# Last group of W_down by eight plain products, and the first group's weight sums behind the norm

## The chip, the cores and the metric

The kernel runs on one core of a Trainium2 chip. The metric is device time in microseconds: the median of three executions. One further execution was recorded by the hardware profiler; all rows below come from that one.

## The reference, cut to what matters

Two decoder layers over 512 tokens of width 1024. Each layer mixes tokens (layer 0: differential and sparse attention, layer 1: forgetting attention), projects, adds and normalises, and then does the same with an MLP. What the change touches is the end of this:

```
x = layer_norm(ALPHA * x + mix, ...)                                   # first norm of a layer
x = layer_norm(ALPHA * x + square(relu(x @ w_up)) @ w_down, ...)       # second norm
```

`w_up` is 1024 x 4096 and `w_down` 4096 x 1024 per layer, all in float32. A float32 operand is used on TensorE as two parts, `hi` (rounded by ScalarE) and `lo` (the rest, a subtraction on VectorE or GpSimd), and a product is three matmuls: hi·hi, hi·lo, lo·hi.

## The kernel before, in words

Tokens lie in four tiles of 128; `xt_[t]` holds tile t of the residual stream with tokens on partitions, and `xTh`/`xTl` hold its transpose, split in two parts, which the projections read. The four engines have their own queues, worked off in order. The order inside each queue is not written by hand: a scheduler replays the program with a timing model of its own and queues, on each engine, what it finds ready, with the order of the source as the tie-break. A tile (a named buffer) that is asked for waits until one of its tag's buffers is free. All DMAs are issued from SyncE's queue (SP).

`out_proj` (L331) makes the first norm's input. Its second half (L355 to L363) goes token tile by token tile: for each t two PSUM banks (tag g, two buffers) of 24 matmuls of 256 columns, each drained by VectorE into `xt_[t]` (L361) with its statistics (L362), then `layer_norm`. Before that loop it already loads and splits the first half-chunk of W_up, `us0` (L346).

`layer_norm` (L207) aggregates the statistics on VectorE, takes the inverse root on GpSimd (L213), and normalises the two halves of the row: half 0 on VectorE (L223, L224), half 1 for tiles 0 to 2 on ScalarE and GpSimd (L219 to L221), for tile 3 on VectorE. Each half is then transposed on TensorE (L124) and split into `xTh`/`xTl` (L114 on ScalarE, L116 on VectorE), or, after the last norm, sent to the output.

`mlp` (L375) has four groups. In each, `up` makes two blocks of 512 hidden features (16 accumulations of 24 matmuls for the pair, in four half-chunks of weights; the first half-chunk of the first block reads tokens 0 to 383 and then 384 to 511), and `down` multiplies them with 1024 rows of W_down. `down` uses Winograd's form of Strassen's scheme: with H and W as 2 x 2 blocks, seven block products in place of eight, at the price of sums of blocks on VectorE: `left(r)` for H (L428 to L438), `right(r)` for W (L450 to L454, `wds` and `wdr` are the tiles). Every operand of a product is split in two (L407/L408 for W, L412/L413 for H). Products r = 3, 6, 7, 5, 1, 2, 4 run in that order, each for two row tiles tt; `evac` adds each to the rows of `xt_` it belongs to, or, for r = 3, to `E`, which goes into three of the four quarters at the very end (L495, last group alone). In the last group the products 2 and 4, which complete tiles 2 and 3, come last; the norms of tiles 0 and 1 are written ahead of them, those of 2 and 3 behind.

The W splits of W_up use tags `whi` and `wlo` (four buffers each) and the raw tag `wraw` (two buffers); W_down's raw blocks use `wdr` (eight buffers). After layer 0's second norm, layer 1 begins with a projection of 272 columns (`nat_chunk`, L181 to L183), 24 matmuls per token tile, whose weights come as three units through the same `wraw`, `whi` and `wlo`, the `lo` part on GpSimd (L146).

Of the kernel before, what the change touches and what calls it, by code (L numbers as in the profile page):

```python
# [15 lines left out]
P = 128  # L16
# [44 lines left out]
def tile_trunk(ctx: ExitStack, tc: tile.TileContext, x, xt_in, ln_gain, ln_bias, w_up, w_down, w_ie, w_oe, lam_p, subln,  # L61
# [46 lines left out]
    def new_xT():  # L108
        for k in range(2):
            xTh[k], xTl[k] = big(F32R), big(F32R)  # L110

    def split(src, hi, lo, scale=1.0):

        A.activation(hi, src, AF.Copy, scale=scale)  # L114
        if scale == 1.0:
            V.tensor_tensor(lo, src, hi.bitcast(F32), op=ALU.subtract)  # L116
        else:
            V.scalar_tensor_tensor(lo, src, scale, hi.bitcast(F32), op0=ALU.mult, op1=ALU.subtract)

    def transpose_x(t, half):  # L120
        b = bank("t")
        for k in range(4):
            c = (half * 4 + k) * P
            T.transpose(b[:, k * P:(k + 1) * P], xt_[t][:, c:c + P], ident)  # L124
        bv = b.rearrange("p (k c) -> p k c", k=4)
        split(bv, xTh[half][:, :, t * P:(t + 1) * P], xTl[half][:, :, t * P:(t + 1) * P])


    lo_engine, rope_engine = [V], [V]
# [77 lines left out]
    def layer_norm(pl, t, st, gb, bb, last=False, spill_to=None):  # L207
        y = xt_[t]
        mv = new(pl, "mv", [P, 2], bufs=2)
        V.bn_aggr(mv, st)  # L210
        ve = new(pl, "ve", [P, 2], bufs=2)
        V.tensor_scalar(ve[:, 0:1], mv[:, 1:2], EPS, None, op0=ALU.add)  # L212
        G.tensor_tensor(ve[:, 1:2], ve[:, 0:1], nhalf[:, 0:1], op=ALU.pow)  # L213
        if t < 3:
            V.tensor_scalar(ve[:, 0:1], mv[:, 0:1], ve[:, 1:2], -1.0, op0=ALU.mult, op1=ALU.mult)
        for hf in range(2):
            cs = slice(hf * 512, (hf + 1) * 512)
            if hf == 1 and t < 3:
                A.activation(y[:, cs], y[:, cs], AF.Identity, bias=ve[:, 0:1], scale=ve[:, 1:2])  # L219
                G.tensor_tensor(y[:, cs], y[:, cs], gb[:, cs], op=ALU.mult)  # L220
                G.tensor_tensor(y[:, cs], y[:, cs], bb[:, cs], op=ALU.add)  # L221
            else:
                V.scalar_tensor_tensor(y[:, cs], y[:, cs], mv[:, 0:1], gb[:, cs], op0=ALU.subtract, op1=ALU.mult)  # L223
                V.scalar_tensor_tensor(y[:, cs], y[:, cs], ve[:, 1:2], bb[:, cs], op0=ALU.mult, op1=ALU.add)  # L224
            if last:
                nc.sync.dma_start(out=out[t * P:(t + 1) * P, cs], in_=y[:, cs])
            else:
                transpose_x(t, hf)
                if spill_to is not None:
                    nc.sync.dma_start(out=spill_to[t * P:(t + 1) * P, cs], in_=y[:, cs])  # L230


    def stacks_q(ap, b, scale):
# [91 lines left out]
    def out_proj(pl, wo, mh, ml, kbs, ln, wu):  # L325

        for n in range(4):
            h, l = wo.take(256)
            for t0 in (0, 2):
                b = bank("g")  # L330
                bv = b.rearrange("p (b c) -> p b c", b=2)  # L331
                for tt in range(2):
                    ts_ = slice((t0 + tt) * P, (t0 + tt + 1) * P)
                    for k, kb in enumerate(kbs[:4]):
                        T.matmul(bv[:, tt], mh[kb][:, ts_], h[:, k], start=k == 0, stop=False)
                        T.matmul(bv[:, tt], mh[kb][:, ts_], l[:, k], start=False, stop=False)
                        T.matmul(bv[:, tt], ml[kb][:, ts_], h[:, k], start=False, stop=k == 3)
                for tt in range(2):
                    y = xt_[t0 + tt][:, n * 256:(n + 1) * 256]
                    V.scalar_tensor_tensor(y, y, ALPHA, bv[:, tt], op0=ALU.mult, op1=ALU.add)  # L340
        stats = [new(pl, f"st{t}", [P, 12]) for t in range(NT)]
        us = [wo.take(256) for _ in range(4)]
        us0 = wu.chunk(256, *[tuple(new(pl, tag, [P, 2, 2, 256], F32R, bufs=3).rearrange("p a b c -> p (a b c)")
                                    for tag in ("sh", "sl")) for _ in range(2)])
        new_xT()
        for t in range(NT):  # L346
            ts_ = slice(t * P, (t + 1) * P)
            for n in range(2):
# [12 lines left out]
                V.tensor_tensor(y, y, b, op=ALU.add)  # L361
                V.bn_stats(stats[t][:, n * 6:(n + 1) * 6], y)  # L362
            layer_norm(pl, t, stats[t].rearrange("p (a b) -> p a b", b=6), *ln)  # L363
        return us0

# [4 lines left out]

    def mlp(mp, wu, wd, us0, ln, last):  # L375
        stats = [new(mp, f"mst{t}", [P, 12]) for t in range(NT)]
        E = [new(mp, f"e{tt}", [P, 512]) for tt in range(2)]
        wdv = wd.flat.rearrange("(h c f p j e) -> h f p c j e", h=2, c=4, f=4, p=P, j=2)
# [1 line left out]
        def up(m):  # L380

            h = big()
            for j in range(2):
                us = us0 if m == 0 and j == 0 else wu.chunk(256, engs=(V, V))
# [30 lines left out]
        def down(g, hs, end):  # L415
# [64 lines left out]
            def evac(r, b, tt):  # L480
                y11, y12, y21, y22 = [Y(i, jd, tt) for i in range(2) for jd in range(2)]
                if r == 3:
                    if g == 0:
                        V.tensor_copy(E[tt], b)
                    else:
                        V.tensor_tensor(E[tt], E[tt], b, op=ALU.add)
                    return
                y = {6: y11, 7: y12, 5: y12, 1: y11, 2: y21, 4: y22}[r]
                op = ALU.subtract if r in (6, 7) else ALU.add
                if g == 0 and r in (6, 7, 2, 4):  # L490
                    V.scalar_tensor_tensor(y, y, ALPHA, b, op0=ALU.mult, op1=op)
                else:
                    V.tensor_tensor(y, y, b, op=op)
                if end and r in (5, 1, 4):
                    V.tensor_tensor(y, y, E[tt], op=ALU.add if r == 1 else ALU.subtract)  # L495

            def norm(t):
                for n in range(2):
                    V.bn_stats(stats[t][:, n * 6:(n + 1) * 6], xt_[t][:, n * 512:(n + 1) * 512])
# [3 lines left out]
            for r in (3, 6, 7, 5, 1) if end else (3, 6, 7, 5, 1, 2, 4):  # L503
                lf, us = left(r), right(r)
                for tt in range(2):
                    evac(r, product(r, lf, us, tt), tt)
            if end:
                if not last:
                    new_xT()
                rest = [(r, left(r), right(r)) for r in (2, 4)]  # L510
                for tt in range(2):
                    norm(tt)
                for tt in range(2):
                    for r, lf, us in rest:
                        evac(r, product(r, lf, us, tt), tt)
                    norm(2 + tt)

        for g in range(4):
            hs = [up(2 * g + m) for m in range(2)]
            down(g, hs, g == 3)  # L520


    def rope(ap, v, cos, sin, heads, bc):
# [473 lines left out]
    for layer in range(DEPTH):  # L997
        mh, ml, kbs, wo, src = (even_layer, odd_layer)[layer]()
        load_x(src)
        with ExitStack() as st:  # L1000
            mp = pool(f"mid{layer}", st)
            wu, wd = Weights(w_up[layer]), Weights(w_down[layer])
            ln = load_ln(mp, layer, 0)
            us0 = out_proj(mp, wo, mh, ml, kbs, ln, wu)
            ln = load_ln(mp, layer, 1)
            mlp(mp, wu, wd, us0, ln, layer == DEPTH - 1)


# [85 lines left out]
```

## Time and profile before

| | us |
|---|---|
| median of three executions | 1325.02 |
| lowest, highest | 1324.26, 1325.5 |
| the profiled execution | 1328.86 |
| its span, first to last instruction | 1326.7 |

Times in the rows are microseconds from the start of the span unless marked ns. PE is TensorE, DVE VectorE, ACT ScalarE, POOL GpSimd. "L12" is line 12 of the kernel before. A line of a timeline gives start, duration, engine, source line, operation, output <- input, count, and in brackets how long the engine had been idle and what released it. Matmuls are pipelined, so their durations overlap; the distance of their starts is what they cost.

### The profile page before, as it was taken

What the parts mean: (1) busy time and instruction counts of PE and PEld (TensorE: products, weight loads), DVE (VectorE), ACT (ScalarE), POOL (GpSimd) and SP (SyncE); (2) the same over time, 40 slices, a digit from 0 to 9 for tenths busy, and PEclk for the clock granted to TensorE, in tenths of its full rate; (3) what the DMA queues carried; (4) which work ended last, traced back from release to release, by engine and by line L of the source; (5) the groups of instructions that cost most, each with busy time, mean ns of one, the idle gap of its engine ahead of it and who ended that gap; (6) DMA issues with size and microseconds to landing.
All of it is one profiled execution on the core that took longest, in us unless ns stands there. A gap on an engine that the chain in (4) does not pass through costs nothing.

```text
span 1326.7 us, 18415 instructions
## 1 busy us (share of the span) xinstructions
PE 1245.3 (94%) x6998; PEld 1087.3 (82%) x6998; DVE 943.0 (71%) x1670; ACT 667.1 (50%) x1209; POOL 310.8 (23%) x321
## 2 busy tenths in 40 slices
PE   7999998999699999999978999999879999999994
PEld 7999896988688888888867789989868888888883
DVE  5467768786639578495796778878745947659488
ACT  5257767752245354454533576666325445354451
POOL 1135654454100000000054354556410000000003
PEclk9999998998799999999988999999979999999997
DMA  7321011225213405234022322232621431514201
GB/s 273 118 83 50 33 48 33 87 60 203 96 33 111 134 28 173 64 115 133 0 80 85 116 88 88 88 124 89 217 95 33 143 112 43 180 32 143 80 1 63
DMA packets 46760, 125.15 MB, mean 94 GB/s; under 512 B 4673, under 2 KB 5185, under 8 KB 46673
## 3 DMA queue, kind: packets, MB, share of 16 engines
q1 hardware_dynamic: 46672, 123.99, 28.4%
q8 instruction: 55, 0.90, 0.3%
q14 instruction: 33, 0.26, 0.1%
HBM read 119.75 MB, written 4.23 MB: 93 GB/s over the span
## 4 chain that ended last, share of the span: by engine, by line
PE 79%; DVE 7%; issue 5%; DMA 4%; POOL 3%; ACT 2%; SPq 0%; POOLq 0%; ACTq 0%; DVEq 0%
PE g L196 10%; PE g L194 10%; PE g L195 10%; PE g L181 4%; PE g L183 4%; PE g L182 4%; PE s L472 3%; PE s L473 3%; PE s L474 3%; PE t L288 3%; DMA wdr<-w_down 2%; PE o L473 2%; PE o L474 2%; PE t L472 2%; PE o L472 2%
## 5 line engine op out<-in xcount | busy, mean ns | idle before, releaser
L195 PE MATMUL g<-big,wlo 128*128 128x512 f32 x608 | 236.7, 391 | 0.0
L194 PE MATMUL g<-big,whi 128*128 128x512 f32 x608 | 236.6, 391 | 0.0
L196 PE MATMUL g<-big,whi 128*128 128x512 f32 x608 | 236.3, 390 | 0.0
L146 POOL TENSOR_TENSOR wlo<-wraw,whi 128x1024 fp32r<-128x1024 f32 (+2 forms) x51 | 126.3, 2481 | 428.8 <-ACT whi L145 416.4
L145 ACT ACTIVATE whi<-wraw 128x1024 fp32r<-128x1024 f32 (+3 forms) x120 | 125.1, 1045 | 130.5 <-DMA wraw<-w_up 45.6
L146 DVE TENSOR_TENSOR wlo<-wraw,whi 128x1024 fp32r<-128x1024 f32 (+2 forms) x69 | 84.5, 1227 | 138.8 <-ACT whi L145 138.8
L408 DVE TENSOR_TENSOR wlo<-wdr,whi 128x1024 fp32r<-128x1024 f32 x96 | 116.3, 1216 | 59.2 <-ACT whi L407 59.2
L407 ACT ACTIVATE whi<-wdr 128x1024 fp32r<-128x1024 f32 x96 | 101.3, 1055 | 64.3 <-PE t L474 37.6
L196 PEld LDWEIGHTS g<-big,whi 128*128 128x128 f32 x608 | 114.3, 188 | 23.6
L194 PEld LDWEIGHTS g<-big,whi 128*128 128x128 f32 x608 | 114.3, 188 | 23.5 <-issue 0.4
L195 PEld LDWEIGHTS g<-big,wlo 128*128 128x128 f32 x608 | 114.3, 188 | 23.1
L181 PE MATMUL g<-whi,big 128*128 128x256 f32 (+2 forms) x416 | 122.0, 293 | 1.4 <-ACT big L114 1.1
L183 PE MATMUL g<-whi,big 128*128 128x256 f32 (+2 forms) x416 | 121.8, 293 | 0.2 <-DVE ve L212 0.2
L182 PE MATMUL g<-wlo,big 128*128 128x256 f32 (+2 forms) x416 | 120.5, 290 | 0.0
L389 ACT ACTIVATE big<-g 128x512 f32<-128x512 f32 x64 | 38.3, 599 | 154.9 <-PE g L196 154.9
L275 ACT ACTIVATE p<-p,sm 128x128 f32<-128x128 f32 (+3 forms) x160 | 89.1, 558 | 46.0 <-DVE sm L274 45.0
L213 POOL TENSOR_TENSOR ve<-ve,nhalf 128x1 f32<-128x1 f32 x16 | 15.6, 974 | 362.2 <-DVE ve L212 362.2
L321 POOL TENSOR_TENSOR p<-p,rs 128x128 f32<-128x128 f32 (+2 forms) x108 | 71.4, 687 | 93.2 <-DVE rs L929 40.4
L181 PEld LDWEIGHTS g<-whi,big 128*128 128x128 f32 x416 | 80.6, 194 | 3.6 <-ACT big L114 1.9
L183 PEld LDWEIGHTS g<-whi,big 128*128 128x128 f32 x416 | 80.8, 194 | 1.2 <-DVE ve L212 0.5
L182 PEld LDWEIGHTS g<-wlo,big 128*128 128x128 f32 x416 | 80.7, 194 | 0.5
L116 DVE TENSOR_TENSOR ptl<-t,pth 128x384 fp32r<-128x384 f32 (+1 forms) x108 | 63.0, 595 | 21.9 <-ACT pth L114 21.3
(263 smaller groups left out, 3139.2 us busy)
## 6 DMA issues: line engine op xcount, KB each, us to landing
wraw<-w_up SPq DMA_DIRECT2D x64, 512.0 KB, 3.6
wdr<-w_down SPq DMA_DIRECT2D x64, 512.0 KB, 4.5
wraw<-w_io SPq DMA_DIRECT2D x22, 512.0 KB, 3.2
wraw<-w_ie SPq DMA_DIRECT2D x18, 512.0 KB, 3.5
v<-w SPq DMA_DIRECT2D x8, 512.0 KB, 5.8
wraw<-w_oe SPq DMA_DIRECT2D x8, 512.0 KB, 3.5
cb<-c_dram SPq DMA_DIRECT2D x16, 256.0 KB, 3.3
wraw<-w_oo SPq DMA_DIRECT2D x8, 512.0 KB, 3.2
```

Of the source, the lines that this page charges most:

```text
L145: A.activation(hi[:, c], raw[:, c], AF.Copy)
L146: (eng or lo_engine[0]).tensor_tensor(lo[:, c], raw[:, c], hi[:, c].bitcast(F32), op=ALU.subtract)
L181: T.matmul(bv[:, tt], xh, h, start=first, stop=False)
L182: T.matmul(bv[:, tt], xh, l, start=False, stop=False)
L183: T.matmul(bv[:, tt], xl, h, start=False, stop=last)
L194: T.matmul(b[:, a:e], h[:, cs], xh, start=k == 0, stop=False)
L195: T.matmul(b[:, a:e], l[:, cs], xh, start=False, stop=False)
L196: T.matmul(b[:, a:e], h[:, cs], xl, start=False, stop=k == 7)
L275: A.activation(pv, pv, AF.Exp, bias=sm[:, i:i + 1], scale=-1.0, accum_out=sm[:, 4 + i:5 + i])
L407: A.activation(hi, r, AF.Copy)
L408: V.tensor_tensor(lo, r, hi.bitcast(F32), op=ALU.subtract)
L472: T.matmul(bv, hh, us[m][0][:, k], start=first, stop=False, skip_group_check=True)
```

## The change

Two things change.

First, `transpose_x`, `layer_norm` and `out_proj` return the last VectorE instruction of the first norm, the subtraction L116 of tile 3's second half (`tail`). In the first block's second half-chunk of W_up, and in the first group's `right(r)`, every VectorE instruction gets an ordering edge behind `tail` (`tc.issue_after`). It is an edge in VectorE's queue alone: no semaphore is added, and the DMAs and the ScalarE casts of the same blocks are not held.

Second, groups 0 to 2 keep the seven products, and the last group becomes `down_last`: `E` goes into its three quarters first; the eight H parts and the eight W blocks are split without any sums; then, for each token tile t and each half jd of the output columns, 24 matmuls of 512 columns accumulate in one bank, VectorE adds the bank to `xt_[t]` and takes its statistics, and after both halves `layer_norm` of that tile follows. All split W blocks stay in their buffers until the last tile.

```
-            layer_norm(pl, t, stats[t].rearrange("p (a b) -> p a b", b=6), *ln)
-        return us0
+            tail = layer_norm(pl, t, stats[t].rearrange("p (a b) -> p a b", b=6), *ln)
+        return us0, tail
...
+                elif m == 0:
+                    with tc.issue_after(tail.ins):
+                        us = wu.chunk(256, engs=(V, V))
...
+            for r in (3, 6, 7, 5, 1, 2, 4):
+                lf = left(r)
+                if g == 0:
+                    with tc.issue_after(tail.ins):
+                        us = right(r)
...
+        def down_last(hs):
+            w = raws(3)
+            for tt in range(2):
+                for i, jd in ((0, 0), (0, 1), (1, 1)):
+                    y = xt_[2 * i + tt][:, jd * 512:(jd + 1) * 512]
+                    V.tensor_tensor(y, y, E[tt], op=ALU.add if jd == 0 else ALU.subtract)
+            H, U = {}, {}
+            for m in range(2):
+                for j in range(2):
+                    hi = new(mp, "sh" if m == 0 or j == 0 else "sl", [P, 2, SEQ], F32R, bufs=3)
+                    if m == 0:
+                        lo = new(mp, "sl", [P, 2, SEQ], F32R, bufs=3)
+                        lo = [lo[:, k] for k in range(2)]
+                    else:
+                        lo = [new(mp, f"t{2 + k}", [P, SEQ], F32R, bufs=2) for k in range(2)]
+                    for k in range(2):
+                        split(hs[m][:, 2 * j + k], hi[:, k], lo[k])
+                        H[m, j, k] = hi[:, k], lo[k]
+            for jd in range(2):
+                for m in range(2):
+                    for j in range(2):
+                        hi = new(wp, ("whi", "wlo")[j], [P, UW], F32R, bufs=4)
+                        lo = new(mp, "wdr" if U else "wds", [P, UW], F32R, bufs=8 if U else 2)
+                        split(w[f"{j + 1}{jd + 1}", m], hi, lo)
+                        U[jd, m, j] = [a.rearrange("p (c k e) -> p k c e", c=2, k=2) for a in (hi, lo)]
+            if not last:
+                new_xT()
+            for t in range(NT):
+                ts_ = slice(t * P, (t + 1) * P)
+                for jd in range(2):
+                    b = bank("os"[jd])
+                    bv = b.rearrange("p (c e) -> p c e", c=2)
+                    for m in range(2):
+                        for j in range(2):
+                            wh, wl = U[jd, m, j]
+                            for k in range(2):
+                                hh, hl = [a[:, ts_] for a in H[m, j, k]]
+                                T.matmul(bv, hh, wh[:, k], start=m + j + k == 0, stop=False)
+                                T.matmul(bv, hh, wl[:, k], start=False, stop=False)
+                                T.matmul(bv, hl, wh[:, k], start=False, stop=m + j + k == 3)
+                    y = xt_[t][:, jd * 512:(jd + 1) * 512]
+                    V.tensor_tensor(y, y, b, op=ALU.add)
+                    V.bn_stats(stats[t][:, jd * 6:(jd + 1) * 6], y)
+                layer_norm(mp, t, stats[t].rearrange("p (a b) -> p a b", b=6), *ln, last=last,
+                           spill_to=None if last else spill)
...
+        for g in range(3):
             hs = [up(2 * g + m) for m in range(2)]
-            down(g, hs, g == 3)
+            down(g, hs)
+        down_last([up(6 + m) for m in range(2)])
```

## Rows read from the trace of the kernel before

**Rows 1.** Parts 1 and 4 of the page: busy us and share; the chain.
```profile
span 1326.7 us, 18415 instructions
...
PE 1245.3 (94%) x6998; PEld 1087.3 (82%) x6998; DVE 943.0 (71%) x1670; ACT 667.1 (50%) x1209; POOL 310.8 (23%) x321
...
PE 79%; DVE 7%; issue 5%; DMA 4%; POOL 3%; ACT 2%; SPq 0%; POOLq 0%; ACTq 0%; DVEq 0%
```

**Rows 2.** Windows in the MLP: us; busy (xrecords) per engine; PEclk, DMA.
```profile
440.00:460.00 20.00, 20.00 (x90) 16.57 (x89) 4.91 (x4) 8.05 (x12) 0.00 (x0) 1.00 0.37 115
...
1280.00:1300.00 20.00, 19.85 (x88) 16.11 (x87) 20.00 (x29) 11.09 (x14) 0.00 (x0) 1.00 0.00 1
```

**Rows 3.** Timeline of PE, layer 0, into the MLP: start, us, instruction, [idle].
```profile
323.19 0.60 PE L124 MATMUL t<-ident,big 128*128 128x128 f32 x4
...
326.55 0.63 PE L124 MATMUL t<-ident,big 128*128 128x128 f32 x4 [1.69 <-issue]
...
343.95 1.09 PE L124 MATMUL t<-ident,big 128*128 128x128 f32 x4 [8.43 <-issue]
...
349.22 1.11 PE L124 MATMUL t<-ident,big 128*128 128x128 f32 x4 [1.85 <-POOL big L221]
```

**Rows 4.** DVE by line, layer 0, 320 to 350 us: busy, mean, idle.
```profile
L146 DVE TENSOR_TENSOR wlo<-wraw,whi 128x1024 fp32r<-128x1024 f32 x4 | 4.8, 1214 | 0.3 <-ACT whi L145 0.3
...
L450 DVE TENSOR_TENSOR wds<-wdr,wdr 128x1024 f32<-128x1024 f32 x2 | 3.5, 1761 | 1.9 <-DMA wdr<-w_down 1.9
...
L451 DVE TENSOR_TENSOR wdr<-wdr,wdr 128x1024 f32<-128x1024 f32 x2 | 3.3, 1665 | 0.0
```

**Rows 5.** The same of layer 1, 946 to 975 us.
```profile
L146 DVE TENSOR_TENSOR wlo<-wraw,whi 128x1024 fp32r<-128x1024 f32 x4 | 4.9, 1216 | 0.4 <-ACT whi L145 0.4
...
L450 DVE TENSOR_TENSOR wds<-wdr,wdr 128x1024 f32<-128x1024 f32 x2 | 3.6, 1836 | 0.6 <-DMA wdr<-w_down 0.6
...
L451 DVE TENSOR_TENSOR wdr<-wdr,wdr 128x1024 f32<-128x1024 f32 x2 | 2.3, 1207 | 0.0
```

**Rows 6.** Timeline of ACT: last evacuation of the first W_up half-chunk, both layers.
```profile
366.44 0.60 ACT L389 ACTIVATE big<-g 128x512 f32<-128x512 f32 x1 [2.94 <-PE g L196]
...
990.82 0.60 ACT L389 ACTIVATE big<-g 128x512 f32<-128x512 f32 x1 [3.35 <-PE g L196]
```

**Rows 7.** Windows at layer 0's MLP start: granted clock behind the busy times.
```profile
336.00:345.00 9.00, 1.05 (x4) 0.71 (x4) 8.73 (x17) 2.98 (x4) 1.99 (x3) 0.59 0.45 133
...
345.00:354.00 9.00, 6.42 (x22) 5.48 (x22) 6.70 (x7) 1.79 (x3) 4.09 (x2) 0.50 0.63 215
```

**Rows 8.** Part 5 of the page: the splits of W_down.
```profile
L408 DVE TENSOR_TENSOR wlo<-wdr,whi 128x1024 fp32r<-128x1024 f32 x96 | 116.3, 1216 | 59.2 <-ACT whi L407 59.2
...
L407 ACT ACTIVATE whi<-wdr 128x1024 fp32r<-128x1024 f32 x96 | 101.3, 1055 | 64.3 <-PE t L474 37.6
```

**Rows 9.** Timeline of PE, end of layer 0 and first projection of layer 1.
```profile
691.29 1.08 PE L124 MATMUL t<-ident,big 128*128 128x128 f32 x4 [7.58 <-DVE big L224]
...
718.58 0.39 PE L194 MATMUL g<-big,whi 128*128 128x512 f32 x1
```

**Rows 10.** Window inside that first projection at full clock.
```profile
714.50:718.50 4.00, 4.00 (x34) 4.00 (x33) 1.37 (x4) 2.46 (x4) 0.42 (x1) 1.00 0.00 0
```

**Rows 11.** Timeline of POOL at the end of layer 0.
```profile
684.51 1.83 POOL L146 TENSOR_TENSOR wlo<-wraw,whi 128x544 fp32r<-128x544 f32 x1 [1.65 <-ACT whi L145]
```

**Rows 12.** Timelines of DVE and POOL at the end of layer 1.
```profile
1304.64 2.46 DVE L499 BATCH_NORM_STATS2 mst<-big 128x6 f32<-128x512 f32 x4
...
1308.15 0.69 DVE L493 TENSOR_TENSOR big<-big,s 128x512 f32<-128x512 f32 x1 [0.27 <-PE s L474]
...
1308.82 0.74 DVE L223 SCALAR_TENSOR_TENSOR big<-big,mv,lng 128x512 f32<-128x512 f32 x1
...
1308.97 0.99 POOL L213 TENSOR_TENSOR ve<-ve,nhalf 128x1 f32<-128x1 f32 x1 [335.63 <-DVE ve L212]
...
1322.00 1.59 POOL L221 TENSOR_TENSOR big<-big,lnb 128x512 f32<-128x512 f32 x1
```

More of the change, by code (lines that the diff above doesn't have):

```diff
@@ L115, in split @@
         if scale == 1.0:
-            V.tensor_tensor(lo, src, hi.bitcast(F32), op=ALU.subtract)
-        else:
-            V.scalar_tensor_tensor(lo, src, scale, hi.bitcast(F32), op0=ALU.mult, op1=ALU.subtract)
+            return V.tensor_tensor(lo, src, hi.bitcast(F32), op=ALU.subtract)
+        return V.scalar_tensor_tensor(lo, src, scale, hi.bitcast(F32), op0=ALU.mult, op1=ALU.subtract)
     def transpose_x(t, half):
@@ L125, in transpose_x @@
         bv = b.rearrange("p (k c) -> p k c", k=4)
-        split(bv, xTh[half][:, :, t * P:(t + 1) * P], xTl[half][:, :, t * P:(t + 1) * P])
+        return split(bv, xTh[half][:, :, t * P:(t + 1) * P], xTl[half][:, :, t * P:(t + 1) * P])
     lo_engine, rope_engine = [V], [V]
@@ L227, in layer_norm @@
             else:
-                transpose_x(t, hf)
+                tail = transpose_x(t, hf)
                 if spill_to is not None:
                     nc.sync.dma_start(out=spill_to[t * P:(t + 1) * P, cs], in_=y[:, cs])
+        return None if last else tail
     def stacks_q(ap, b, scale):
@@ L362, in out_proj, with mlp @@
                 V.bn_stats(stats[t][:, n * 6:(n + 1) * 6], y)
-            layer_norm(pl, t, stats[t].rearrange("p (a b) -> p a b", b=6), *ln)
-        return us0
-    def mlp(mp, wu, wd, us0, ln, last):
+            tail = layer_norm(pl, t, stats[t].rearrange("p (a b) -> p a b", b=6), *ln)
+        return us0, tail
+    def mlp(mp, wu, wd, us0, tail, ln, last):
         stats = [new(mp, f"mst{t}", [P, 12]) for t in range(NT)]
@@ L383, in up @@
             for j in range(2):
-                us = us0 if m == 0 and j == 0 else wu.chunk(256, engs=(V, V))
+                if m == 0 and j == 0:
+                    us = us0
+                elif m == 0:
+                    with tc.issue_after(tail.ins):
+                        us = wu.chunk(256, engs=(V, V))
+                else:
+                    us = wu.chunk(256, engs=(V, V))
                 for nb in range(2):
@@ L413, in hsplit, with down @@
             V.tensor_tensor(lo, src, hi.bitcast(F32), op=ALU.subtract)
-        def down(g, hs, end):
+        def down(g, hs):
             H = [[[h[:, 2 * j:2 * j + 2, 256 * i:256 * i + 256] for j in range(2)] for i in range(2)] for h in hs]
@@ L493, in evac @@
                     V.tensor_tensor(y, y, b, op=op)
[L494 to L499, printed above, removed]
+            for r in (3, 6, 7, 5, 1, 2, 4):
[3 more added lines that the diff above has]
+                        us = right(r)
+                else:
+                    us = right(r)
+                for tt in range(2):
+                    evac(r, product(r, lf, us, tt), tt)
@@ new lines, in down_last @@
+        def down_last(hs):
+            w = raws(3)
+            for tt in range(2):
+                for i, jd in ((0, 0), (0, 1), (1, 1)):
[8 more added lines that the diff above has]
+                        lo = [lo[:, k] for k in range(2)]
+                    else:
+                        lo = [new(mp, f"t{2 + k}", [P, SEQ], F32R, bufs=2) for k in range(2)]
[27 more added lines that the diff above has]
+                    V.bn_stats(stats[t][:, jd * 6:(jd + 1) * 6], y)
@@ L500, in norm @@
                 layer_norm(mp, t, stats[t].rearrange("p (a b) -> p a b", b=6), *ln, last=last,
                            spill_to=None if last else spill)
[L503 to L516, printed above, removed]
@@ L518, in mlp @@
-        for g in range(4):
+        for g in range(3):
             hs = [up(2 * g + m) for m in range(2)]
-            down(g, hs, g == 3)
+            down(g, hs)
+        down_last([up(6 + m) for m in range(2)])
     def rope(ap, v, cos, sin, heads, bc):
@@ L1003, in tile_trunk @@
             ln = load_ln(mp, layer, 0)
-            us0 = out_proj(mp, wo, mh, ml, kbs, ln, wu)
+            us0, tail = out_proj(mp, wo, mh, ml, kbs, ln, wu)
             ln = load_ln(mp, layer, 1)
-            mlp(mp, wu, wd, us0, ln, layer == DEPTH - 1)
+            mlp(mp, wu, wd, us0, tail, ln, layer == DEPTH - 1)
 def _constants():
```

## The prediction, made blind

> **What bounds the kernel now.** I read the page first, then windows of 20 us over the whole span, then the timelines of the stretches in which TensorE has a gap. TensorE is busy for 1245.3 of the span's 1326.7 us, and the chain that ended last runs for 79% of the span through it [rows 1]. The reader is to see two kinds of stretch. Inside the MLP TensorE is full: 90 matmuls of 512 columns in 20.00 us, one per 0.222 us, and the same rate while VectorE too is busy all of the time [rows 2]. There, only the number of matmuls counts; a faster VectorE gives nothing. At four places TensorE stands still for a norm: at the start of each layer's MLP, at the end of layer 0, and at the end of the kernel. The change adds matmuls to the full stretch and touches all four gaps.
>
> **Added: matmuls of the last group.** Seven products of 2 x 12 matmuls are 168; four token tiles, two halves, 24 each are 192. 24 more at 0.222 to 0.227 us are 5.4 us per layer, 10.8 us in all, on the path in full.
>
> **Added and removed beside it, costed at nothing.** The last group's W splits fall from 14 blocks to 8: 8 x 1.06 us on ScalarE and 8 x 1.22 us on VectorE [rows 8], 8.4 and 9.7 us within the group's new 192 x 0.222 = 43 us; all block sums go. What hides them is `up`. The four blocks of the first output half take the weight buffers that the second block's first half-chunk gives back, half a block (48 matmuls, 10.9 us) before the products start, and need about 5 us of VectorE by then. The other four come free at the start of the products and are wanted 24 matmuls, 5.4 us, later, one per six matmuls (1.4 us). VectorE makes one in 1.2 us, so this just holds; if it doesn't, the price is a wait of 1 to 3 us per layer. I take 0.
>
> **Moved: the weight sums and subtractions at the start of the MLP.** In layer 0 VectorE ran four sums (3.5 + 3.3 us) and four subtractions of W_up (4.8 us) between the steps of the first norm, and stood 1.9 us waiting for W_down's transfer with the norm queued behind: 13.5 us, some 0.3 us less for the overlap of neighbours [rows 4]. In layer 1 it is 3.6 + 2.3 + 4.9 + 0.6 + 0.4 = 11.8 us [rows 5]. Four of these eight instructions per layer are subtractions, two of them of the next block; these aren't in the ordered blocks, but follow, as their raw data waits for one of two buffers that the first two give back. [...]
>
> With the moved work gone, what is late next is tile 2's second half. TensorE has its sums ready at 324.9 us (the 1.69 us of idle before 326.55 begin there [rows 3]). Sum, statistics and aggregate 1.7 us, inverse root 1.0 [rows 12], ScalarE's half row (taken like VectorE's, 0.74), GpSimd's two steps (1.6 each) [rows 12], transposes (0.60) [rows 3], split (0.60 like rows 6 and 0.69 like a sum [rows 12]), eight hand-overs of some 0.2: about 336 us. The first block then runs from 336 and not, after its false start, from the transposes at 349.22 [rows 3]. That would be 13 us or more, and a gap of some 4 us in place of 8.43 should leave less time at half clock. Against it stand the removed work as a cap on what VectorE's queue can give back (13.2 and 11.8 us) and a schedule that will not be ideal. I take 12 us for layer 0 and 11 us for layer 1. The bounds: 4 us each if another link (GpSimd's two steps, tile 3's own norm) holds TensorE nearly as long; 17 us each if the half clock goes with the gap. The marker is the last evacuation of the first half-chunk, at 366.44 and 990.82 us [rows 6].
>
> What waits for the moved work now: the second half-chunk's two subtractions (2.4 us behind the tail), wanted by TensorE only 96 matmuls after the block starts, some 12 us. SyncE's queue: W_up's next two raw blocks can be fetched only when these two have run, some 3 to 4 us later than now, and are wanted a whole block (22 us) later. The sums are for products 40 us away. All hidden; the price without that cover is what they cost now.
>
> **Moved: the norms at the end of layer 0.** Before, all four tiles complete in the last few microseconds of the products. TensorE's last product ends at 683.71 (691.29 less the 7.58 idle), and the next layer's first projection ends at 718.58 [rows 9]: 34.9 us, with 96 matmuls in it that take 4.00 / 34 = 0.12 us each at full clock [rows 10], some 12 us, and eight transposes. After, tiles 0 to 2 are normalised, transposed and split under the 10.9 us of the next tile's products. What is left behind the last matmul is tile 3: sum, statistics, aggregate 1.7 us, inverse root 1.0, four half-row steps of 0.74 [rows 12], transposes and split: 9 to 10 us, beside which the projection of tiles 0 to 2 (9 us) runs. Its weights: three units, of which GpSimd makes the short one in 1.83 us [rows 11], a long one by its size in 2.75. Now all three can be split only in the last 5.4 us, as the W blocks keep their buffers until tile 3; the third is ready some 4 to 5 us behind the last matmul. I put the end of the projection 16 us behind the last matmul: 34.9 - 16 = 18.9, less 5.4 added, a net gain of 13.5 us. Bounds 7 (GpSimd's splits hold tile 3's inverse root, half clock) and 15.
>
> **Moved: the norms at the end of the kernel.** The last sum starts at 1308.15, the last GpSimd step ends at 1323.59, and the span at 1326.7 [rows 12]: 15.4 us of four tiles' norms in a heap, 3.1 of transfer. After: sum and statistics 1.2 us, aggregate 0.3, inverse root 1.2 with a half-row step under it, two or three more at 0.7, some 4.3 us. 15.4 - 4.3 = 11.1, less 5.4, a net gain of 5.7. Bounds 3 and 7.
>
> **TensorE's queue in the last group.** Three tiles' transposes now stand between products of layer 0, and TensorE waits for them if they are placed too early. The same pattern is in `out_proj`, where it cost 1.69 us over the loop [rows 3]. I take 2 us. [...]
>
> **The sum.** -12 - 11 - 13.5 - 5.7 + 2 = -40.2 us, the 10.8 us of added matmuls included in the third and fourth terms. The profiled execution took 1328.86 us, 2.2 more than its span and 0.29% above the median of 1325.02. It would become 1288.7; against the median, 1325.02 - 40.2 = 1284.8 us.
>
> **Rivals.**
> *The starts give little.* VectorE's queue is cleared, but GpSimd's chain of tile 2 and tile 3's own norm end almost as late, and the clock is at half again. For it: the 1.85 us of idle before 349.22 ended at GpSimd's L221, not at VectorE [rows 3]. Against: that GpSimd step itself had waited for the VectorE steps ahead. With 4 us at each start: -8 - 13.5 - 5.7 + 2 = -25, 1300 us.
>
> [...]
>
> *The change doesn't do what it says.* If the edges only reorder what was late anyway, the starts give 0: -13.5 - 5.7 + 2 = -17, 1308 us. Against: all of the moved work was ahead of L116 in the queue, with no idle time but the transfer's [rows 4].
>
> **How the numbers follow.** My forecast has 0.66, the first rival 0.16, the third 0.07, the slower one 0.07; for a last group that loses just what the norms give, within 0.2% (2.65 us, what a measurement of this kernel can tell from no change), 0.04. Faster is 0.66 + 0.16 + 0.07 = 0.89. The forecast's own range comes from the bounds: at best -17 - 17 - 15 - 7 = -56, at worst -4 - 4 - 7 - 3 + 6 = -12; as they won't meet at one end, I take 1270 to 1304, which holds the first rival's time as well and leaves out the third and the slower one.
>
> **What would show it.** The evacuations of rows 6 some 11 to 12 us earlier against the start of their `out_proj`; no L450 or L451 on VectorE before the last L116; 192 matmuls in the last group at 0.222 us with no gap above 2 us; at most 17 us from the last product of layer 0 to the end of the first projection; about 8 us from the last matmul to the end of the span. I would be wrong if TensorE's gap at the start of the MLP stays above 6 us, or if gaps open between the token tiles.

## The result and the profile after

The changed kernel takes **1273.05 us** (median of 4 runs, 1272.16 to 1273.65) against 1325.26 (1324.26 to 1326.95) for the kernel before in the same session: ratio 0.9604, 95% interval 0.9588 to 0.9621. That is 52.2 us faster; 40.2 were forecast. A second set of runs gave 1275.20 us, ratio 0.9620 (0.9603 to 0.9636). Two slow executions are left out of what follows: 1373.98 us of `sums_only`, and 4320.5 us of the kernel before in the same session.

Parts 1 and 4 of the page after, against [rows 1]: TensorE is busy for 7.8 us less, although it runs 48 more matmuls, so part of its busy time before was slow time (mean granted clock over the span 0.964 before, 0.994 after). VectorE loses 65 us.
```profile
span 1271.5 us, 18398 instructions
...
PE 1237.5 (97%) x7046; PEld 1079.2 (85%) x7046; DVE 878.2 (69%) x1602; ACT 647.3 (51%) x1185; POOL 301.2 (24%) x321
...
PE 86%; DVE 6%; DMA 3%; ACT 2%; issue 1%; POOL 1%; SPq 0%; DVEq 0%; ACTq 0%; POOLq 0%
...
L414 DVE TENSOR_TENSOR wlo<-wdr,whi 128x1024 fp32r<-128x1024 f32 x72 | 87.4, 1218 | 44.4 <-ACT whi L413 44.4
...
L413 ACT ACTIVATE whi<-wdr 128x1024 fp32r<-128x1024 f32 x72 | 75.9, 1055 | 48.2 <-PE t L480 29.6
```
The last two lines answer to [rows 8]: 12 splits per layer fewer, and two more per layer from `wds`, which [rows 8] and these lines leave out. The last group's eight now run through `split` (L116), so eight stand for 14.

**The start of layer 0's MLP.** TensorE's timeline, against [rows 3]: the 8.43 us gap is gone. TensorE stands for 1.00 us, runs four matmuls of `up`, transposes tile 2's second half at 330.61, and then has matmuls without a break.
```profile
328.10 0.60 PE L123 MATMUL t<-ident,big 128*128 128x128 f32 x4
329.70 0.44 PE L193 MATMUL g<-big,sh 128*128 128x384 f32 x1 [1.00 <-ACT big L114]
...
330.61 0.66 PE L123 MATMUL t<-ident,big 128*128 128x128 f32 x4
...
337.18 1.03 PE L123 MATMUL t<-ident,big 128*128 128x128 f32 x8
```
VectorE's timeline, against [rows 4]: the sums (L456, L457) and the subtractions (L145) now stand behind the norm's last step, L116 at 338.45.
```profile
338.45 1.29 DVE L116 TENSOR_TENSOR big<-t,big 128x512 fp32r<-128x512 f32 x2 [4.50 <-ACT big L114]
339.65 2.35 DVE L145 TENSOR_TENSOR wlo<-wraw,whi 128x1024 fp32r<-128x1024 f32 x2
341.92 2.35 DVE L456 TENSOR_TENSOR wds<-wdr,wdr 128x1024 f32<-128x1024 f32 x2
344.19 2.35 DVE L457 TENSOR_TENSOR wdr<-wdr,wdr 128x1024 f32<-128x1024 f32 x2
```
Windows of the same place, against [rows 7] (the granted clock is the third number from the end): 1.00 where 0.59 and 0.50 stood.
```profile
336.00:345.00 9.00, 9.00 (x74) 8.97 (x73) 6.55 (x7) 2.15 (x4) 0.00 (x0) 1.00 0.42 124
345.00:354.00 9.00, 9.00 (x41) 7.45 (x41) 3.81 (x4) 4.93 (x8) 0.00 (x0) 1.00 0.44 142
```
ScalarE's evacuations, against [rows 6], are 20 us (layer 0) and 49 us (layer 1) earlier on the clock of the span; counted from token tile 1 of their `out_proj`'s second half it is 17.2 and 15.8 us, for the forecast's 11 to 12.
```profile
346.02 0.58 ACT L395 ACTIVATE big<-g 128x512 f32<-128x512 f32 x1
...
941.53 0.58 ACT L395 ACTIVATE big<-g 128x512 f32<-128x512 f32 x1
```

**The last group and the ends.** TensorE's timeline in layer 0: tile 0's transposes at 643.76 stand among the products of the next tile, with no idle time; behind the last product (670.46) it stands twice for 0.4 us, and the next layer's first projection ends at 685.13, 14.7 us behind, against 34.9 [rows 9].
```profile
643.76 0.60 PE L123 MATMUL t<-ident,big 128*128 128x128 f32 x4
...
677.34 1.29 PE L123 MATMUL t<-ident,big 128*128 128x128 f32 x8 [0.39 <-DVE big L223]
679.03 0.36 PE L180 MATMUL g<-whi,big 128*128 128x272 f32 x1 [0.41 <-DVE fz L946]
...
685.13 0.40 PE L193 MATMUL g<-big,whi 128*128 128x512 f32 x1
```
VectorE at the end of the kernel, against [rows 12]: one tile's norm, 4.6 us, where four stood.
```profile
1263.71 0.69 DVE L553 TENSOR_TENSOR big<-big,s 128x512 f32<-128x512 f32 x1 [4.13 <-PE s L551]
...
1266.87 1.41 DVE L223 SCALAR_TENSOR_TENSOR big<-big,ve,lnb 128x512 f32<-128x512 f32 x2
```

**Where the 55.2 us between the two spans lie,** by markers on TensorE and ScalarE: 3.2 ahead of token tile 1 in the second half of layer 0's `out_proj` (its 49th matmul), a stretch which the change doesn't touch (the profile before had more half clock there, see the last section); **18.1** from there to the third evacuation of `up` (layer 0's start); 12.1 from there to the end of layer 1's first projection (20.2 less behind the last product, 8.1 more in the products); 0.0 in layer 1's attention; **16.8** at layer 1's start; 4.9 to the end (10.8 less behind the last product, 5.9 more ahead of it). Without the untouched stretch it is 52.0, which is what the runs show.

### The profile page after: what moved, and what is told of

Its sections match the earlier page's. It is cut to its first block, busy times and chain, and to the rows that moved or that the text cites. A ratio compares the mean times of both kernels' runs of the same rounds, so it can differ in the third digit from the quotient of the medians.

```text
span 1271.5 us, 18398 instructions
## 1 busy us (share of the span) xinstructions
PE 1237.5 (97%) x7046; PEld 1079.2 (85%) x7046; DVE 878.2 (69%) x1602; ACT 647.3 (51%) x1185; POOL 301.2 (24%) x321
## 4 chain that ended last, share of the span: by engine, by line
PE 86%; DVE 6%; DMA 3%; ACT 2%; issue 1%; POOL 1%; SPq 0%; DVEq 0%; ACTq 0%; POOLq 0%
PE g L193 11%; PE g L194 11%; PE g L195 11%; PE g L180 4%; PE g L181 4%; PE g L182 4%; PE s L478 3%; PE t L288 3%; PE s L479 3%; PE s L480 2%; DMA wraw<-w_up 2%; PE s L270 2%; PE o L480 2%; PE t L478 2%; PE o L478 2%; PE o L479 2%
## 5 line engine op out<-in xcount | busy, mean ns | idle before, releaser
L145 DVE TENSOR_TENSOR wlo<-wraw,whi 128x1024 fp32r<-128x1024 f32 (+2 forms) x69 | 84.3, 1228 | 96.5 <-ACT whi L144 96.4
L145 POOL TENSOR_TENSOR wlo<-wraw,whi 128x1024 fp32r<-128x1024 f32 (+2 forms) x51 | 123.4, 2425 | 94.6 <-ACT whi L144 82.3
L180 PE MATMUL g<-whi,big 128*128 128x256 f32 (+2 forms) x416 | 120.3, 289 | 0.6 <-DVE fz L946 0.4
L182 PE MATMUL g<-whi,big 128*128 128x256 f32 (+2 forms) x416 | 119.6, 287 | 0.0
L414 DVE TENSOR_TENSOR wlo<-wdr,whi 128x1024 fp32r<-128x1024 f32 x72 | 87.4, 1218 | 44.4 <-ACT whi L413 44.4
L413 ACT ACTIVATE whi<-wdr 128x1024 fp32r<-128x1024 f32 x72 | 75.9, 1055 | 48.2 <-PE t L480 29.6
L180 PEld LDWEIGHTS g<-whi,big 128*128 128x128 f32 x416 | 79.1, 190 | 2.2 <-ACT fv L114 0.6
L182 PEld LDWEIGHTS g<-whi,big 128*128 128x128 f32 x416 | 79.1, 190 | 0.7 <-issue 0.4
L116 DVE TENSOR_TENSOR ptl<-t,pth 128x384 fp32r<-128x384 f32 (+1 forms) x108 | 63.1, 595 | 21.1 <-ACT pth L114 20.4
```

What stands on the lines that cost most here:

```text
L145: (eng or lo_engine[0]).tensor_tensor(lo[:, c], raw[:, c], hi[:, c].bitcast(F32), op=ALU.subtract)
L180: T.matmul(bv[:, tt], xh, h, start=first, stop=False)
L182: T.matmul(bv[:, tt], xl, h, start=False, stop=last)
L413: A.activation(hi, r, AF.Copy)
L414: V.tensor_tensor(lo, r, hi.bitcast(F32), op=ALU.subtract)
```

## The experiments

### Each half of the change alone

`order_only` keeps the last group of before and adds the two waits; `last_only` is the changed kernel without them:
```diff
 # order_only (both layers): seven products in the last group, but
+    with tc.issue_after(tail.ins): us = wu.chunk(256, engs=(V, V))   # m == 0, j == 1
+    with tc.issue_after(tail.ins): us = right(r)                     # g == 0
 # last_only: down_last as in the change, but
-    with tc.issue_after(tail.ins): ...
```


> Only the ordering edges of the change: the next half-chunk's subtractions and the first group's sums of W_down behind the preceding norm, in both layers; the last group stays seven products as before. Theory: the edges alone made the two starts shorter, by 18.1 us in layer 0 and 16.8 us in layer 1 of the two profiles, so about 1325 - 35 = 1290 us, and TensorE's clock stays at 1.00 behind out_proj. Rival: the starts gain only the 23 us of the forecast (1302 us), and the other 12 us of the result belong to the new last group (its buffers, and transfers that start earlier). The point between them is 1296 us.

Measured 1289.89 us, ratio 0.9732 (0.9718 to 0.9745): 35.2 us from the waits alone. In its profile the two starts are 41.2 and 41.9 us long (59.7 and 58.4 before, see the table below), so they account for all of it.

> Only the new last group: eight plain products, token tile by token tile, with the norms between them; no ordering edges, so both starts of the MLP stay as before. Theory: the end of layer 0 gives 12.2 us net and the end of the kernel 4.9 us net, 17 us, so about 1308 us, and with the edges' 35 us it adds up to the whole change's 52 us. Rival: the two parts help each other (the edges give buffers and transfers an earlier start), then this alone gives less than 12 us and the sum of both parts stays below 47 us.

Measured 1310.74 us, ratio 0.9890 (0.9877 to 0.9904): 14.3 us, a little under the 17. The product of the two ratios is 0.9625; the whole change had 0.9604 and 0.9620. The halves add up, and neither needs the other.

### Each wait alone

```diff
 # chunk_only: only the subtractions of W_up wait     # sums_only: only the sums of W_down wait
-    with tc.issue_after(tail.ins): us = right(r)      -    with tc.issue_after(tail.ins): us = wu.chunk(...)
```


> The changed kernel with one of its two ordering edges: the next half-chunk's subtractions of W_up wait for the preceding norm, the first group's sums of W_down don't. The two edges together gave 35.2 us. Theory: both kinds of moved work stood in VectorE's queue between the norm's steps, so each gives back in proportion to its time there: subtractions 4.8 of 13.2 us in layer 0 and about as much in layer 1, so this edge alone gives 35.2 x 0.38 = 13 us and leaves the kernel some 22 us above the changed one, at about 1295 us. Rival: the gap closes only when the last late step goes, so that one edge alone gives little (under 6 us: above 1302 us) and the two together more than their parts.

> The changed kernel with the other edge alone: the sums of W_down for the first group wait for the norm, the subtractions of W_up don't. Theory: in proportion to VectorE's time (8.4 of 13.2 us, the wait for the transfer included) it gives 35.2 x 0.62 = 22 us and leaves the kernel some 13 us above the changed one, at about 1286 us. Rival: the sums are nearly all of it (over 30 us, below 1278 us), because only they wait for a transfer with the norm behind them.

Measured 1301.11 us (0.9823; 0.9809 to 0.9837) and 1280.58 us (0.9670; 0.9651 to 0.9689). Against `last_only`, which has neither, that is 9.6 and 30.2 us; shares by VectorE's time would have been 13 and 22. Both kernels also lose 3.2 us in layer 1's attention, which they don't touch (222.6 and 222.5 us for 219.4; see `less24`), so the starts alone are to be compared: by the table below they are 11.3 us shorter in `chunk_only` than in `last_only`, 31.2 in `sums_only`, and 35.2 with both waits. The sums' wait by itself gives nine tenths, as its rival said, and the two parts alone add up to more than both give together. That the transfer is the reason, as that rival has it, is not shown. TensorE's timeline of `chunk_only` still has a long gap, its window the half clock:
```profile
337.04 1.09 PE L123 MATMUL t<-ident,big 128*128 128x128 f32 x4 [5.07 <-issue]
```
```profile
336.00:345.00 9.00, 6.52 (x24) 5.24 (x25) 7.59 (x10) 2.61 (x4) 4.00 (x4) 0.54 0.32 118
```
The same in `sums_only`: gaps of 0.69 and 1.02 us, and the full clock.
```profile
330.28 0.44 PE L195 MATMUL g<-big,sh 128*128 128x384 f32 x1 [1.02 <-DVE big L116]
```
```profile
336.00:345.00 9.00, 8.69 (x69) 8.28 (x68) 6.58 (x8) 2.01 (x4) 0.00 (x0) 1.00 0.46 160
```

### The gap filled, the wait left

```diff
 # warm: the kernel before, in out_proj behind the last product
+                with tc.issue_after(mm.ins):
+                    for _ in range(36):
+                        T.matmul(b, mh[kbs[0]][:, 0:P], mh[kbs[0]], start=True, stop=True)
```


> The kernel before, with 36 extra matmuls of 512 columns per layer into a bank that nobody reads, right behind out_proj's last product: 36 x 0.22 = 8 us of TensorE work in the place where TensorE stood idle for 8.43 us. VectorE's queue stays as it was, and so does the time at which the first block's inputs are ready. [...] Rival: the start is bounded by VectorE's queue throughout, and a faster clock there gives only another wait: 0 to -2 us, or slower by what the extra matmuls hold up.

Measured 1322.74 us, ratio 0.9982 (0.9974 to 0.9991): 2.4 us faster by the ratio, near the rival's end; the author's estimate for a clock that stays at 1.00 was 10 us. TensorE works through the former gap, and the window that had 0.50 has 0.81:
```profile
334.47 7.31 PE L367 MATMUL s<-big 128*128 128x512 f32 x31
...
345.66 0.44 PE L196 MATMUL g<-big,sh 128*128 128x384 f32 x1 [1.79 <-DVE big L116]
```
```profile
345.00:354.00 9.00, 8.34 (x42) 8.01 (x43) 3.80 (x7) 1.69 (x3) 1.13 (x1) 0.81 0.42 150
```
In the profile the two starts are 3.1 and 1.8 us shorter, 5 in all, and everything from there on is as before; why the timed runs show only half of it stays open (the execution behind the profile before took 1328.86 us, 3.8 more than the median). So extra work can buy back part of the clock, but the waiting itself has to go.

### The first block made to wait for tile 2's second half

The forecast had the first block start only when this half is there, at 336 us. In the changed kernel it starts earlier, on the first halves. Here the same matmuls run in the other order:
```diff
 # second_first, tr_block, first half-chunk only
-            for k in range(8):
+            for k in (4, 5, 6, 7, 0, 1, 2, 3):
```


> The changed kernel with one thing altered in each layer: the first block of the MLP (token tiles 0 to 2 in one piece, tile 3 in another, two output blocks) takes the second half of the model's columns before the first, with the same matmuls. So TensorE can't start it before tile 2's second half is there, which is what the forecast had assumed. [...] If the second half is there as early as the first, nothing is lost: 1273 us, and the forecast's 336 us was itself wrong.

Measured 1279.94 us, ratio 0.9662 (0.9644 to 0.9680), 4.7 us above the changed kernel beside it. The author's estimates of the loss were 7 us without a half clock behind the wait and 12 us with one; there is none, and each start carries only 1.7 us. The profile has another 3.1 us in layer 1's attention, where the scheduler placed other instructions. TensorE's timeline: three waits of 2.26 us together, and the clock stays at 1.00.
```profile
332.04 0.66 PE L123 MATMUL t<-ident,big 128*128 128x128 f32 x4 [1.15 <-POOL big L220]
333.38 0.44 PE L193 MATMUL g<-big,sh 128*128 128x384 f32 x1 [0.69 <-ACT big L114]
...
334.77 0.45 PE L195 MATMUL g<-big,sh 128*128 128x384 f32 x1 [0.42 <-DVE big L116]
```
Counted from token tile 1 of `out_proj`'s second half, 334.77 here is 335.8 in the profile before: the forecast's 336. The time of that half was right, and the early start on first halves is worth 1.7 us.

**A sum that holds in all of these.** From token tile 1 of `out_proj`'s second half to the third evacuation of `up` (whose pair of blocks has 8 accumulations of 24 matmuls, not the 16 of the description of the kernel): idle is the stretch less TensorE's busy time; clock is the sum over slices of 1 us of busy time x (1 - granted clock); the rest is work at full clock (of `warm` less its 36 x 0.222 = 8.0 us). In layer 0 it runs from 312.23 to 371.95 before, and from 309.00 to 350.65 after:
```profile
312.23 0.39 PE L357 MATMUL g<-whi,big 128*128 128x256 f32 x1 [0.31 <-DVE big L361]
...
371.95 0.60 ACT L389 ACTIVATE big<-g 128x512 f32<-128x512 f32 x1 [4.26 <-PE g L196]
```
```profile
309.00 0.39 PE L357 MATMUL g<-whi,big 128*128 128x256 f32 x1 [0.30 <-DVE big L361]
...
350.65 0.60 ACT L395 ACTIVATE big<-g 128x512 f32<-128x512 f32 x1 [2.58 <-PE g L195]
```
All stretches, in us:

| kernel | layer 0: length = idle + clock + rest | layer 1 |
|---|---|---|
| before | 59.7 = 12.9 + 5.7 + 41.1 | 58.4 = 13.2 + 4.3 + 40.9 |
| last_only | 59.7 = 12.9 + 5.7 + 41.1 | 58.8 = 13.4 + 4.6 + 40.9 |
| warm, less 8.0 | 48.6 = 5.2 + 1.7 + 41.7 | 48.5 = 5.6 + 1.5 + 41.4 |
| chunk_only | 54.0 = 9.7 + 2.9 + 41.4 | 53.2 = 8.7 + 3.5 + 40.9 |
| sums_only | 43.3 = 2.0 + 0.0 + 41.3 | 44.0 = 2.4 + 0.0 + 41.6 |
| second_first | 43.2 = 2.3 + 0.0 + 41.0 | 43.5 = 2.5 + 0.0 + 41.0 |
| after | 41.7 = 1.0 + 0.0 + 40.7 | 41.6 = 1.1 + 0.0 + 40.5 |

The rest stays between 40.5 and 41.7, so idle and clock carry the differences.

### The last group: overlap, matmuls, order

```diff
 # norms_late: the changed kernel, down_last
-                layer_norm(mp, t, ...)                    # behind each tile
+            with tc.issue_after(end.ins):                 # the last tile's bn_stats
+                for t in range(NT): layer_norm(mp, t, ...)
```


> The changed kernel, but the norms of all four token tiles of the last group wait until the last tile's statistics are there; the products, splits and sums stay as they are. Theory: what the last group gives at its ends is that three norms lie under the next tile's products. Without that, layer 0 pays again the 34.9 - 14.7 = 20 us less 2.6 us of transposes that leave the products' stretch, and the kernel's end 18.6 - 7.8 = 11 us: +28 us, about 1301 us. Rival: the gain comes from VectorE and ScalarE, which have 14 blocks to split before and 8 now and no block sums, and are free when the last product ends; then late norms cost half or less, +14 us, 1287 us. The point between them is 1294 us.

Measured 1299.89 us, ratio 0.9809 (0.9796 to 0.9823): 26.8 us lost, some 3 of them in layer 1's attention (222.5 us for 219.4): nearer the theory's 28 than the rival's 14. TensorE waits for the heap of norms again:
```profile
673.84 1.12 PE L123 MATMUL t<-ident,big 128*128 128x128 f32 x4 [5.40 <-DVE big L223]
...
678.63 0.59 PE L182 MATMUL g<-whi,big 128*128 128x272 f32 x1 [2.17 <-DVE big L116]
```
From the last product to the end of the first projection it is 29.2 us (14.7 in the changed kernel, 34.9 before), behind the kernel's last product 18.5 (7.8, and 18.6 before). VectorE has eight blocks to split and no sums here too. So the overlap makes 14.5 of the 20.2 us at layer 0's end and nearly all of the 10.8 at the kernel's. The other 5.7 us at layer 0's end are there without it; what gives them is not shown.

```diff
 # pool_lo: order_only, last group
-            V.tensor_tensor(lo, r, hi.bitcast(F32), op=ALU.subtract)
+            (G if end and m else V).tensor_tensor(lo, r, hi.bitcast(F32), op=ALU.subtract)
```


> The kernel before with the two ordering edges, the last group still seven products with its norms in two pairs, but the low parts of half of the last group's split weight blocks made on GpSimd in place of VectorE. This measures the rival for the ends: that VectorE's relief in the last group, not the tile by tile order, made its gain. Rival: with about 8 us of VectorE's subtractions gone from the last group, the kernel gains at least half of the 17 us that separate the edges alone (1290 us) from the changed kernel, that is below 1282 us. Theory: VectorE is not what the ends wait for until the last sums are there; no gain, 1288 to 1292 us, or slower where GpSimd is late with a block.

Measured 1293.87 us, ratio 0.9770 (0.9753 to 0.9786): 4.0 us slower than the waits alone. It is no test of the rival, as VectorE got no relief. In layer 0's last group 7 of 14 subtractions went to GpSimd, where they take 18.2 us; but VectorE's other steps grew beside them, and over the products it was busy for 37.73 of 38.64 us in `order_only` and 43.58 of 44.91 here (the third busy time of the windows). `order_only`:
```profile
624.05:662.69 38.64, 38.48 (x169) 31.27 (x167) 37.73 (x53) 20.34 (x27) 6.11 (x2) 1.00 0.03 8
L419 DVE TENSOR_TENSOR sl<-t,sh 128x512 fp32r<-128x512 f32 x6 | 4.0, 687 | 0.0
```
`pool_lo`:
```profile
624.66:669.57 44.91, 40.48 (x171) 32.63 (x170) 43.58 (x52) 21.33 (x28) 20.97 (x10) 0.96 0.02 7
L419 DVE TENSOR_TENSOR sl<-t,sh 128x512 fp32r<-128x512 f32 x6 | 9.5, 1593 | 0.1
```
The products now stand for blocks. In layer 0 that makes them 6 us longer, which the stretch behind the last product gets back (27.5 us for 34.0); in layer 1 it makes them 4 us longer, and nothing comes back:
```profile
643.44 0.47 PE L478 MATMUL s<-whi,sh 128*128 128x512 f32 x1 [2.30 <-ACT sh L418]
...
661.94 0.50 PE L479 MATMUL s<-wlo,sh 128*128 128x512 f32 x1 [2.12 <-DVE wlo L414]
```

```diff
 # less24: the changed kernel, down_last; tiles 0 to 2 without hl x wh of the first block
+    if m or t == 3:
         T.matmul(bv, hl, wh[:, k], start=False, stop=m + j + k == 3)
```


> The changed kernel without the low-part products of the first 1024-row block of the last group for token tiles 0 to 2 (8 matmuls in each of the tiles, 24 per layer, 48 in all; the output lacks these small terms). All else stays. Theory: TensorE is full in the last group, so each matmul there is on the path: 48 x 0.224 = 10.8 us less, 1262 us. Rival: the tile by tile order leaves slack behind splits or norms that hides some of them; then less than 6 us are saved, above 1267 us.

Measured 1264.82 us, ratio 0.9541 (0.9528 to 0.9554): 8.2 us saved, between the two. The products' stretch is 5.6 us shorter in layer 0 and 5.5 in layer 1, all of the 48 x 0.23; 3.3 us come back in layer 1's attention (222.7 us for 219.4), behind a wait that the changed kernel doesn't have; `chunk_only`, `sums_only`, `second_first` and `norms_late` wait around there too:
```profile
711.12 0.50 PE L270 MATMUL s<-nka,q 128*128 128x512 f32 x1 [2.08 <-DVE sm L274]
```

```diff
 # tile_wait: the changed kernel, layer 0's down_last
+    with tc.issue_after(tr[0].ins):     # TensorE's last transpose of the tile before
         for jd in range(2): ...         # the products of this tile
```


> The changed kernel, but in layer 0's last group each token tile's products wait in TensorE's queue until the tile before it has been transposed (no other instruction is added or left out). [...] Worked out from the changed kernel's trace: tile 0's last product ends at about 635.8 us and GpSimd ends its second half at 642.6 us, then one transpose of 0.6 us: 7.4 us of wait per tile, 22 us for three. [...] Theory 2: the transposes that now lie inside other work are only moved and the clock recovers at once: 20 to 24 us, 1296 us. [...]

Measured 1297.91 us, ratio 0.9797 (0.9774 to 0.9820), 23 to 25 us above the changed kernel's two results: theory 2's number, by another road. TensorE stands in front of both halves' transposes, the same for each of the three tiles:
```profile
639.70 1.11 PE L123 MATMUL t<-ident,big 128*128 128x128 f32 x4 [3.91 <-DVE big L223]
642.57 1.11 PE L123 MATMUL t<-ident,big 128*128 128x128 f32 x4 [1.76 <-POOL big L220]
```
```profile
633.00:643.00 10.00, 4.33 (x18) 3.04 (x18) 5.32 (x10) 1.41 (x2) 3.52 (x3) 0.81 0.07 26
643.00:653.00 10.00, 10.00 (x40) 8.12 (x39) 2.08 (x3) 0.60 (x1) 0.00 (x0) 0.84 0.08 28
```
Idle is 17.1 us in all (5.7 per tile, not 7.4) and the clock costs 7.2 by the same sum, so the clock did not recover at once (0.84 in the second window). Products that were ready waited 3.91 us behind a transpose here.

### A version that might be faster

`after_again` is the changed kernel unaltered, to stand beside it; `v_chain` takes GpSimd's subtractions off the stretch in which TensorE waits longest:
```diff
 # v_chain: the first weight chunks of layer 1's attention
-            us = wi.chunk(w)
+            us = wi.chunk(w, engs=(V, V, V))
```


> The changed kernel once more, unaltered, to stand beside the two kernels that run with it. By its first runs 1273 us (1271 to 1275), 52 us below the kernel before; a difference of under 3 us between this run and those says how far apart two kernels have to lie to be told apart here.

> A version that may beat the changed kernel: in each layer the low parts of the first weight blocks that follow the first projection are made on VectorE in place of GpSimd. In the changed kernel TensorE's largest remaining gap in layer 1 is 2.79 us in front of the forget gates' sums, whose VectorE steps (2.27 and 2.33 us for what takes a fraction of that elsewhere) lie beside a 4.74 us GpSimd subtraction. Theory: the two engines hold each other up there; with the subtraction on VectorE the steps are short, the gap and the 0.87 clock behind it go, and the kernel gains 2 to 4 us. Rival: VectorE is the busier engine in this stretch (9.9 of 12 us), so the subtractions push other steps back: 0, or some us slower.

Measured 1275.20 us (0.9620; 0.9603 to 0.9636) and 1279.43 us (0.9656; 0.9642 to 0.9671): 4 us slower, as the rival allowed. (The edit is in layer 1 alone.) In the changed kernel GpSimd's two subtractions take 4.74 us, and VectorE's tiny steps beside them 2.27 and 2.33 us:
```profile
691.88 4.74 POOL L145 TENSOR_TENSOR wlo<-wraw,whi 128x1024 fp32r<-128x1024 f32 x2 [2.49 <-ACT whi L144]
```
```profile
691.57 0.20 DVE L1000 TENSOR_SCALAR fq<-fq 128x64 f32<-128x64 f32 x1
...
692.06 2.27 DVE L1000 TENSOR_SCALAR fq<-fq 128x64 f32<-128x64 f32 x1
694.37 2.33 DVE L999 TENSOR_TENSOR fq<-fq,fs 128x64 f32<-128x64 f32 x1
```
In `v_chain` each such step takes 0.19 to 0.23 us and TensorE's 2.79 us gap is gone, as the theory said; but layer 1's attention takes 226.4 us for 219.4, with 4.0 us more idle and 1.4 more lost to the clock, the largest wait now further on (2.14 us, for a softmax step of VectorE). Whether VectorE's load does that, or another order of the queues as in the kernels above, is not shown. No version tried that computes the whole of it beats the changed kernel.

## Why the forecast was right, and where it was short

**The step that was mis-sized is "I take 12 us for layer 0 and 11 us for layer 1".** Measured: 18.1 and 16.8, 11.9 us short in all, which is the whole miss (52.2 - 40.2 = 12.0); the time lies 3 us above the lower end of the range. The forecast capped each start at what the removed work had taken in VectorE's queue, 13.2 and 11.8 us, and both gave more. By the table, TensorE's idle time fell by 11.9 and 12.1 us, so the forecast's numbers are the size of the idle time alone, though it had not worked them out from that. The other 5.7 and 4.3 us are what TensorE's work in these stretches had lost at a lower granted clock: in layer 0 as [rows 7] show, 1.7 us of it from 327 to 331 us (0.50 to 0.65) already, in layer 1 at 0.50 from 963 to 979 us. The prediction, with [rows 7] before it, named 17 us as the bound "if the half clock goes with the gap", and left it out of the value, since it expected a gap of some 4 us to remain. Two things were wrong in that. The gap is 1.00 us, as `up` starts on the columns whose norm is ready; and `second_first`, which undoes just this, has 2.3 us of waits in pieces and no half clock either. Its start is still 16.5 us shorter than before. So the larger error was to leave the clock in, not the overlooked early start.

**Added matmuls: right.** The products' stretches grew by 8.1 and 5.9 us. 5.4 are the matmuls; in layer 0 a further 2.2 us are the transposes that moved in between (the stretch is that much shorter in `norms_late`, where they stay behind). `less24` saves 5.6 and 5.5 us there: on the path in full.

**Splits beside them, at nothing: right.** 192 matmuls run in layer 1's last group at 0.23 us each with no gap.

**End of layer 0: right.** 14.7 us behind the last product for 16, net 12.1 for 13.5 less 2 for the transposes. `norms_late` shows that the overlap makes 14.5 of the 20.2 us; for the other 5.7 no mechanism is shown.

**End of the kernel: right.** Net 4.9 for 5.7; 7.8 us behind the last matmul for "about 8".

**TensorE's queue: cheaper than taken.** No wait at all at the transposes; the scheduler places them a tile later. The slower rival was that each tile's transposes stand right behind its own products; its 50 us were the author's estimate, 11.7 us of waiting and 5 of clock for each of three tiles. Such a place does cost, but less: `tile_wait` puts it at 23 to 25 us, as TensorE waits 5.7 us per tile and the clock costs 2.4. Even so the kernel would have been faster than before. The 8.43 us of [rows 3] show only that TensorE stood in front of a transpose: the matmul behind it (345.73 us) needed that transpose's split, with 0.69 us of idle until ScalarE's L114. `tile_wait` shows ready products held up, for 3.91 us.

**The other rivals.** The starts did not "give little", and the waits do what they say (`order_only`). That only the moved work ahead of L116 mattered is right in kind; `sums_only` shows that the sums' part of it gives nine tenths.

## What to carry to other kernels

When a wait in front of TensorE is taken away, count two terms: the idle time, and the busy time behind it x (1 - granted clock); here the second was a third of the gain at layer 0's start. Put norms of finished tiles under the next tile's products, and read from the trace where the transposes stand in TensorE's queue, for placed right they cost no wait and, for three tiles placed a tile earlier, some 24 us. Expect a small edit to move the order far away: five kernels here lost 3 us in an attention stage that they don't touch, so compare the stage that was edited and not only the total.

## What the runs showed of the hardware

What the clock cost differed with the form of the gap. By the sum above, 5.7 us were lost at granted clocks down to 0.50 around the 8.43 us gap of layer 0 and its neighbours [rows 3, 7], 2.9 around one of 5.07 us (`chunk_only`), 2.4 per tile around two of 3.91 and 1.76 us with a transpose between (`tile_wait`), and nothing around pieces of 1.15, 0.69 and 0.42 us (`second_first`). Each figure is from one trace, and the loss also changes from one execution to the next: one gap of 2.11 us in layer 0's `out_proj`, with the same matmuls around it, came with 4.4 us of lost clock in the profile before (granted 0.50 for 9 us), 1.6 in the profile after (0.50 for 2 us), and none in `after_again` (1.00), which is the changed kernel once more.

A VectorE step of 0.20 us took 2.27 us while GpSimd ran a subtraction of 2.37 us (4.74 for two), and the next 2.33 us under the second; with those subtractions on VectorE none of them took more than 0.23 us. In `pool_lo` a step of 0.69 us took 1.59 on the mean beside GpSimd's subtractions. In the changed kernel the two long steps ended within 0.1 us of the two GpSimd instructions; what held them is not shown.
